# The attention scale moved from the softmax into the weight column of the query latent's norm

## The chip, the core and the metric

The kernel runs on one core of one Trainium2 chip. The metric is the device time of one execution in microseconds; the figure of a kernel is the median of its runs. The engines are named as in the profile: PE is the matrix engine (PEld its weight load), DVE the vector engine, ACT the scalar engine, POOL and SP the two others, of which SP issues most of the DMAs.

## The reference

Two decoder layers on a sequence of 1024 tokens of width 1024, in fp32. Layer 0 is an mLSTM mixer and an MLP; layer 1 is multi-head latent attention and an MLP. The part that matters here is the attention of layer 1: a latent of the query (384 wide) is normalised with a learned weight, projected to 8 heads of 128 plain and 64 rotary columns, and compared with the keys; the scores are scaled, masked and put through a softmax.

```python
cq = rmsnorm(h @ w_q_a, g_q_latent)
q = (cq @ w_q_b).reshape(B_, S, B_HEADS, B_NOPE + B_ROPE)
...
scale = (B_NOPE + B_ROPE) ** -0.5
...
s = (jnp.einsum('bqhd,bkhd->bhqk', qn_b, k_nope)
     + jnp.einsum('bqhd,bkd->bhqk', qr_b, k_rope)).astype(jnp.float32) * scale
s = jnp.where(kpos[None, :] <= qpos[:, None], s, -jnp.inf)
p = jax.nn.softmax(s, axis=-1)
```

## The kernel before

The sequence is worked in two halves of 512 tokens. Nearly every product is done in three passes of a reduced format (a number is split into a high and a low part): `mm3` (L279 to L282) issues high by high, high by low and low by high into the same bank. `wsplit` makes the two parts of a weight, with a cast on ACT (L238) and a subtraction on DVE (L239); `split_mod` does the same for activations (L499 and L500).

From about 990 us on, the attention of one half of the sequence is woven with the MLP of another: `two_streams` (L2771) takes steps of a dense stream (MLP products) and of the other stream (the mixer of layer 1) in turn. Each step's instructions on PE are tied behind the last PE instruction of the step before (`tc.issue_after` in `go`, L2754), so that the order on PE is largely written by hand. What DVE, ACT and the DMA queue on SP do in between is put in order by a planner when the kernel is built (`schedule_with_timeline_sim=True`, L2934): it plays the program through with estimated durations, and gives each engine the ready instruction of the best priority. The priority follows the order of tracing; what is wrapped in `prompt` (L244) or `evac` goes 300 places ahead (`PRIO`). An instruction that is traced late but ready early may so run far ahead of its place.

The query latent `cq` is made in `latent` (L1605): three projections, a reciprocal root mean square (`rstd`), and at L1706 the product with `col(QL + m, 1)` and `rstd`. `col` cuts columns out of the tile `cols`, into which L330 turns the learned vectors at the start; columns 194 to 196 (`QL`) hold `g_q_latent`, one column for 128 of its 384 entries. The split latent then goes through the projections of `kq`, `rot` (first half) or `prepare_pair` (second half) to the plain and the rotary queries, and in `score_mm` (L1770) to the scores: four products of the parts (L1781 to L1784), the mask as a product of an identity with `maskA` (L1786; -1e30 where a key is hidden), and the high by high product (L1787). The scores of one block of 128 queries stay in a bank pair `pm` of PSUM, of which there are two; the MLP uses the same two.

`softmax` (L1789) runs on 128 queries by n keys: a row maximum, negated (L1791, DVE); its product with the scale (L1792, DVE, 128 x 1); the exponential with the scale as immediate factor and the product as bias, which also sums (L1793, ACT); the reciprocal of the sum (L1794) and the product with it (L1795, both DVE). `scores` (L1797) calls it 64 times, under `prompt`: for the first half (`attention_first`, n from 128 to 512, two softmaxes to one `pm`) and for the second (`attention_second`, n from 640 to 1024, one to a `pm`). The result is turned in blocks of 128 by PE (L1901, L1915, L1988) and multiplied with the values.

`rope_perm` (L1521) fills three permutation matrices in `selW` on DVE (L1524 to L1526) from the identity. It is traced once (L2842), after the stretch that works beside the last sweep of the MLP of layer 0 and ahead of both attentions.

Of the kernel before, what the change touches and what calls it, by code (L numbers as in the profile page):

```python
# [13 lines left out]
AF = mybir.ActivationFunctionType  # L14
ALU = mybir.AluOpType
# [67 lines left out]
def kernel(  # L83
# [27 lines left out]
    nc = tc.nc  # L111
# [32 lines left out]
    def small(n, dt=F32):  # L144
        return sb.tile([P, n], dt, tag=f"sm{n}", bufs=6, name=f"sm_{next(uid)}")
# [7 lines left out]
    def pm():  # L153
        return pp.tile([P, 2, 512], F32, tag="pm", bufs=2, name=f"pm_{next(uid)}")
# [177 lines left out]
    col = lambda i, n: cols[:, i : i + n]  # L332
    NG = lambda l, i: col(l * 32 + i * 8, 8)
    AB, KVB, KVG, HG, KVL, QL, GB = 64, 160, 176, 184, 192, 194, 197
# [1184 lines left out]
    both, both_perm = selW[:, 1], selW[:, 2]  # L1519

    def rope_perm():  # L1521
        for q in range(4):
            s = ts(q, 32)
            nc.vector.tensor_copy(perm[:, s], ident[:, ts(q ^ 1, 32)])  # L1524
            nc.vector.tensor_add(both[:, s], ident[:, s], ident[:, ts(q ^ 2, 32)])
            nc.vector.tensor_add(both_perm[:, s], ident[:, ts(q ^ 1, 32)], ident[:, ts(q ^ 3, 32)])  # L1526
# [186 lines left out]
    SCALE = float((128 + 64) ** -0.5)  # L1713
# [75 lines left out]
    def softmax(f, pr, n):  # L1789
        m, l = small(1), small(1)  # L1790
        nc.vector.reduce_max(m, f, axis=AX.X, negate=True)  # L1791
        nc.vector.tensor_scalar(m, m, SCALE, None, ALU.mult)  # L1792
        nc.scalar.activation(pr[:, :n], f, AF.Exp, bias=m, scale=SCALE, accum_out=l)  # L1793
        nc.vector.reciprocal(l, l)  # L1794
        nc.vector.tensor_scalar(pr[:, :n], pr[:, :n], l, None, ALU.mult)  # L1795

    def scores(kk, unit):  # L1797

        (_, q, kn, _), j = unit
        prs = []  # L1800
        if j < 2:
            st = pm()
            pr = raw().rearrange("p (a b) -> p a b", b=512)
            for e in range(2):
                score_mm(lambda g: st[:, e], kk, q, kn, 2 * j + e)
            for e in range(2):
                n = (2 * j + e + 1) * P
                prompt(softmax)(st[:, e, :n], pr[:, e], n)
                prs.append(pr[:, e])
        else:  # L1810
            for e in range(2):
                st = pm()
                n = (2 * j + e + 1) * P
                score_mm(lambda g: st[:, g], kk, q, kn, 2 * j + e)
                pr = raw()
                prompt(softmax)(st.rearrange("p a b -> p (a b)")[:, :n], pr, n)
                prs.append(pr)
        return prs
# [598 lines left out]
    m = [pm(), pm()]  # L2417
# [422 lines left out]
    two_streams(f0, behind(bg_latent(), 5))  # L2840
    apart[0] = False
    rope_perm()  # L2842


# [93 lines left out]
```

## Time and profile before

| what | value |
|---|---|
| time, median of 3 runs | 2321.11 us (2319.03 to 2321.47) |
| the profiled execution | 2317.84 us |
| its span, first to last instruction | 2316.1 us |
| granted clock of PE, mean | 0.997 |
| first and last softmax (start of L1791) | 992.9 and 1771.4 us |
| L1791, 64 times, median | 0.754 us |
| L1793, 64 times, median | 0.744 us |

The profile is of one execution, which was 3.27 us shorter than the median of the others. Times in it count from the span's start. "Idle before, released by" names, for each group, what ended the time in which the engine had nothing to do; a wait for several semaphores is put down to the one that came last.

### The profile page before, as it was taken

How to read it: one execution, taken by the hardware profiler on the slowest of the kernel's cores; microseconds unless marked ns; L12 is line 12 of the kernel's file. 1: busy time of each engine (PE TensorE's matmuls, PEld its weight loads, DVE VectorE, ACT ScalarE, POOL GpSimd, SP SyncE). 2: the span in 40 equal slices, each digit the busy share in tenths (PEclk: the TensorE clock that was granted, in tenths of full speed). 3: DMA queues.
4: the chain of work that ended last, by engine and by line, in shares of the span. 5: the costliest groups of instructions: out<-in, count | busy, mean ns of one | idle time of the engine just before them, and what ended most of it. 6: DMA issues, size and time to landing. Idle time of an engine off the chain costs nothing.

```text
span 2316.1 us, 32512 instructions
## 1 busy us (share of the span) xinstructions
PE 2276.3 (98%) x12010; PEld 1918.0 (83%) x12010; DVE 1698.5 (73%) x2782; ACT 1126.6 (49%) x1919; POOL 84.1 (4%) x164
## 2 busy tenths in 40 slices
PE   8999999999999999999999999999999999999998
PEld 6888788888887878778888788888888888989997
DVE  6676777889887877777765687666666388788776
ACT  4365435765334445545444555433444354555453
POOL 1000000001122210000000000000000000000000
PEclk9999999999999999999999999999999999999999
DMA  9543464668999887656775654764324352445432
GB/s 314 180 129 112 135 182 154 196 221 266 329 282 295 284 293 259 195 187 204 242 253 192 225 197 151 254 230 157 129 95 157 107 168 82 153 144 176 125 110 110
DMA packets 401647, 444.36 MB, mean 192 GB/s; under 512 B 27123, under 2 KB 289328, under 8 KB 401488
## 3 DMA queue, kind: packets, MB, share of 16 engines
q1 hardware_dynamic: 388544, 397.09, 53.6%
q0 software_dynamic: 12944, 45.20, 5.3%
q8 instruction: 94, 1.54, 0.3%
q14 instruction: 65, 0.53, 0.1%
HBM read 343.65 MB, written 98.57 MB: 191 GB/s over the span
## 4 chain that ended last, share of the span: by engine, by line
PE 75%; DMA 9%; DVE 9%; issue 4%; ACT 2%; POOL 0%; SPq 0%; DVEq 0%; ACTq 0%; POOLq 0%
PE ps L280 13%; PE ps L282 13%; PE ps L281 13%; PE pm L280 8%; PE pm L281 8%; PE pm L282 8%; DMA raw<-in_mlp_w_dram 4%; PE pc L281 2%; PE pc L280 2%; PE pc L282 2%; DMA raw<-s 1%; DVE wl L239 1%; DVE k L247 1%; PE pc L1988 1%; DVE sm L1791 1%
## 5 line engine op out<-in xcount | busy, mean ns | idle before, releaser
L238 ACT CAST wh<-raw 128x1024 fp32r<-128x1024 f32 (+2 forms) x317 | 321.4, 1016 | 437.2 <-PE ps L281 177.4
L239 DVE TENSOR_TENSOR wl<-raw,wh 128x1024 fp32r<-128x1024 f32 (+2 forms) x317 | 375.3, 1186 | 202.6 <-ACT wh L238 169.9
L280 PE MATMUL ps<-k,wh 128*128 128x512 f32 (+1 forms) x1252 | 476.0, 380 | 4.8 <-DVE tmc L1084 1.4
L282 PE MATMUL ps<-k,wl 128*128 128x512 f32 (+1 forms) x1252 | 468.4, 374 | 0.5 <-DVE wl L239 0.5
L281 PE MATMUL ps<-k,wh 128*128 128x512 f32 (+1 forms) x1252 | 467.9, 374 | 0.0
L280 PEld LDWEIGHTS ps<-k,wh 128*128 128x128 f32 x1252 | 236.2, 189 | 51.9 <-issue 2.8
L282 PEld LDWEIGHTS ps<-k,wl 128*128 128x128 f32 x1252 | 236.0, 189 | 43.4 <-DVE wl L239 1.0
L281 PEld LDWEIGHTS ps<-k,wh 128*128 128x128 f32 x1252 | 236.3, 189 | 41.4 <-issue 1.4
L247 DVE TENSOR_TENSOR k<-k,pm 128x512 f32<-128x512 f32 (+1 forms) x250 | 192.5, 801 | 63.3 <-PE pm L282 62.8
L280 PE MATMUL pm<-wh,hd 128*128 128x512 f32 x488 | 193.5, 396 | 3.5 <-ACT raw L1793 2.3
L282 PE MATMUL pm<-wh,hd 128*128 128x512 f32 x488 | 190.5, 390 | 0.0
L281 PE MATMUL pm<-wl,hd 128*128 128x512 f32 x488 | 190.3, 390 | 0.0
L280 PEld LDWEIGHTS pm<-wh,hd 128*128 128x128 f32 x488 | 91.7, 188 | 25.3 <-ACT raw L1793 4.6
L282 PEld LDWEIGHTS pm<-wh,hd 128*128 128x128 f32 x488 | 91.6, 188 | 19.9 <-DVE hd L500 0.5
L281 PEld LDWEIGHTS pm<-wl,hd 128*128 128x128 f32 x488 | 91.8, 188 | 18.4 <-issue 0.5
L390 DVE SCALAR_TENSOR_TENSOR tma<-raw,cond,tma 128x512 f32<-128x512 f32 x120 | 89.6, 747 | 16.6 <-DMA raw<-in_ada_w_dram 7.8
L281 PE MATMUL pm<-hd,wk 128*128 128x512 f32 x256 | 100.0, 391 | 1.7 <-DVE hd L500 1.7
L1793 ACT ACTIVATE raw<-pm,sm 128x128 f32<-128x128 f32 (+3 forms) x64 | 47.6, 743 | 111.0 <-DVE sm L1792 106.4
L280 PE MATMUL pm<-hd,wk 128*128 128x512 f32 x256 | 100.9, 394 | 0.6 <-ACT hd L499 0.6
L280 PE MATMUL pm<-hd,wh 128*128 128x512 f32 x256 | 99.2, 389 | 1.1 <-ACT hd L499 1.1
L282 PE MATMUL pm<-hd,wl 128*128 128x512 f32 x256 | 99.8, 390 | 0.1
L281 PE MATMUL pm<-hd,wh 128*128 128x512 f32 x256 | 99.6, 390 | 0.2 <-DVE hd L500 0.2
(497 smaller groups left out, 4828.1 us busy)
## 6 DMA issues: line engine op xcount, KB each, us to landing
raw<-in_mlp_w_dram SPq DMA_DIRECT2D x176, 512.0 KB, 4.5
raw<-in_ada_w_dram SPq DMA_DIRECT2D x64, 512.0 KB, 4.6
raw<-in_mlp_w_dram SPq DMA_DIRECT2D x128, 256.0 KB, 4.7
raw<-in_a_w_in_dram SPq DMA_DIRECT2D x44, 512.0 KB, 4.5
lo<-wl POOLq DMA_DIRECT2D x32, 512.0 KB, 6.1
wk<-lo SPq DMA_DIRECT2D x64, 256.0 KB, 4.4
xs<-k SPq DMA_DIRECT2D x40, 256.0 KB, 4.7
raw<-in_a_w_out_dram SPq DMA_DIRECT2D x16, 512.0 KB, 4.9
```

What stands on the lines that cost most here:

```text
L238: nc.scalar.copy(hi[:, :n], r[:, :n])
L239: i = nc.vector.tensor_sub(lo[:, :n], r[:, :n], hi[:, :n].bitcast(F32))
L247: return f(*a, **k)
L280: nc.tensor.matmul(o, lh, rh, start=start, stop=False)
L281: nc.tensor.matmul(o, lh, rl, start=False, stop=False)
L282: pe_last[0] = nc.tensor.matmul(o, ll, rh, start=False, stop=stop)
L390: nc.vector.scalar_tensor_tensor(acc, r[kk], cond[:, k : k + 1], acc, ALU.mult, ALU.add)
L1791: nc.vector.reduce_max(m, f, axis=AX.X, negate=True)
L1793: nc.scalar.activation(pr[:, :n], f, AF.Exp, bias=m, scale=SCALE, accum_out=l)
L1988: nc.tensor.transpose(pt[:, ts(m, P)], u.prs[i][:, ts(kb, P)], ident)
```

## The change

The scale (192 to the power -0.5) is multiplied once into the three `QL` columns, in `rope_perm`; L1706 then gives a latent, and with it queries and scores, that carry it already. The product at L1792 is dropped, the exponential takes the negated maximum as its bias and no scale.

```diff
     def rope_perm():
+        nc.vector.tensor_scalar(col(QL, 3), col(QL, 3), SCALE, None, ALU.mult)
         for q in range(4):
             s = ts(q, 32)
             nc.vector.tensor_copy(perm[:, s], ident[:, ts(q ^ 1, 32)])
...
     def softmax(f, pr, n):
         m, l = small(1), small(1)
         nc.vector.reduce_max(m, f, axis=AX.X, negate=True)
-        nc.vector.tensor_scalar(m, m, SCALE, None, ALU.mult)
-        nc.scalar.activation(pr[:, :n], f, AF.Exp, bias=m, scale=SCALE, accum_out=l)
+        nc.scalar.activation(pr[:, :n], f, AF.Exp, bias=m, accum_out=l)
         nc.vector.reciprocal(l, l)
         nc.vector.tensor_scalar(pr[:, :n], pr[:, :n], l, None, ALU.mult)
```

## The prediction

> **What bounds the kernel now.** I read the top of the page first, then its chain of waits, then who waited for whom on TensorE (PE).
>
> ```profile
> span 2316.1 us, 32512 instructions
> PE 2276.3 (98%) x12010; PEld 1918.0 (83%) x12010; DVE 1698.5 (73%) x2782; ACT 1126.6 (49%) x1919; POOL 84.1 (4%) x164
> PE 75%; DMA 9%; DVE 9%; issue 4%; ACT 2%; POOL 0%; SPq 0%; DVEq 0%; ACTq 0%; POOLq 0%
> ```
>
> PE is busy for 98% of the span and makes up 75% of the chain that ended last. Only 2316.1 - 2276.3 = 39.8 us are PE idle. A change that takes nothing from PE, as this one, can win at most part of these, and only where the softmax is what PE waits for. The waits of PE on the lines of the softmax (L1791 to L1795), and its longest wait of all:
>
> ```profile
> PE pc L280 <- DVE hd L500: 3.7, 1, 3.7
> PE pm L280 <- ACT raw L1793: 2.3, 4, 1.0
> PE pc L1915 <- DVE raw L1795: 1.4, 1, 1.4
> PE pc L1988 <- DVE raw L1795: 1.3, 6, 0.4
> PE ps L280 <- DVE sm L1792: 1.0, 1, 1.0
> PE pc L1901 <- DVE raw L1795: 0.4, 1, 0.4
> ```
>
> The columns are us in total, times, longest. The five softmax rows make 2.3 + 1.4 + 1.3 + 1.0 + 0.4 = 6.4 us in 13 waits: the whole of what a shorter softmax can win directly. That is 0.28% of the span. All other PE work runs beside the softmax without noticing it, although ScalarE (ACT) does notice:
>
> ```profile
> L1792 DVE TENSOR_SCALAR sm<-sm x64: 141/153/156, 993.2 to 1772.7; 128x1 f32<-128x1 f32 x64
>   ACT raw L1793: 106.4, 50
> ```
>
> The exponential sat 106.4 us behind the product, in 50 of 64 cases. That number is tempting and nearly worthless: ACT is busy for 49% of the span, so most of it is an engine with nothing else to do, waiting for the product only because it came last.
>
> **The change part by part.**
>
> 1. Removed: 64 products on VectorE (DVE), 64 x 0.153 = 9.8 us of durations. DVE is busy for 73% and is not the bound, so this is worth only what it takes off the chain reduce, product, exponential. Without anything between, that step reads:
>
> ```profile
> 992.87 0.28 DVE L1791 TENSOR_REDUCE sm<-pm 128x1 f32<-128x128 f32 x1
> 993.19 0.15 DVE L1792 TENSOR_SCALAR sm<-sm 128x1 f32<-128x1 f32 x1
> 993.46 0.37 ACT L1793 ACTIVATE raw<-pm,sm 128x128 f32<-128x128 f32 x1 [4.35 <-DVE sm L1792]
> ```
>
> The reduce ends at 993.15; the exponential starts at 993.46, 0.31 us later. With the reduce releasing it directly, one handover of 0.12 us (993.34 to 993.46) stays: 0.19 us saved for each softmax.
>
> One rule of the Trainium skill would make this term smaller. "Perfetto Trace Analysis", section Optimizing Scalar/DVE Operations, puts the data-access overhead of a DVE instruction on SBUF at about 60 ns of engine time and says that the profiled latency is about twice this. An estimate from that page with 0.06 in place of 0.19 would bring the sum below to 1.3 us; the rows here show the dependent step at 0.15 + 0.04, so the trace decides against using the smaller figure for a chain.
>
> 2. Moved: in some softmaxes the order of DVE holds other work between reduce and product, which now falls behind the reduce's release.
>
> ```profile
> 1562.19 0.82 DVE L1791 TENSOR_REDUCE sm<-pm 128x1 f32<-128x640 f32 x1
> 1562.92 0.68 DVE L500 TENSOR_TENSOR hd<-tmp,hd 128x512 fp32r<-128x512 f32 x1
> 1563.52 0.14 DVE L1792 TENSOR_SCALAR sm<-sm 128x1 f32<-128x1 f32 x1
> ```
> ```profile
> 1564.70 0.50 PE L280 MATMUL pm<-wh,hd 128*128 128x512 f32 x1 [0.55 <-ACT raw L1793]
> ```
> ```profile
> 999.41 0.56 DVE L1791 TENSOR_REDUCE sm<-pm 128x1 f32<-128x384 f32 x1
> ...
> 1001.61 0.14 DVE L1792 TENSOR_SCALAR sm<-sm 128x1 f32<-128x1 f32 x1
> ```
>
> At 1562 the reduce ends at 1563.01 and the product at 1563.66; the exponential could go 0.65 us earlier, more than the 0.55 us for which PE then waits for the score bank, so that wait goes. At 999 the product came 1.64 us after its reduce, and PE did not wait at all: most of such gaps buy nothing.
>
> 3. Added: one DVE product on 128x3 values in rope_perm, as long as L1792's 0.15 us. It reads the columns that L330 writes, and L1706 is its first reader.
>
> ```profile
> L330 DVE COPY cols<-ps x1: 233/233/233, 15.7 to 15.7; 128x72 f32<-128x72 f32 x1
> L1524 DVE CAST selW<-ident x4: 171/172/174, 268.2 to 268.5; 128x32 fp32r<-128x32 f32 x4
> L1706 DVE SCALAR_TENSOR_TENSOR k<-k,cols,tmc x6: 742/745/752, 959.1 to 1431.4; 128x512 f32<-128x512 f32 x6
> 17.77 0.16 DVE L2334 TENSOR_TENSOR ada<-pc,cols 128x2 f32<-128x2 f32 x1 [1.27 <-PE pc L2330]
> ```
>
> L1524, traced in the same function, runs at 268.2 us, far ahead of where it is traced: the planner fills DVE's gaps with any ready instruction. The new product is ready at 15.9 us and I expect it soon after, in a gap such as the 1.27 us ahead of 17.77. Hidden there it costs 0; without that cover 0.15 us. Its reader is on DVE too, over 900 us later: no new wait on another engine. No DMA is added or moved by the edit, and no queue is crossed; the exponential loses an immediate factor and keeps its bias column, so I take its duration as unchanged.
>
> 4. The sum. Pm waits: 0.55 in full and 0.19 for each of the three others, 1.1. L1988: six of 0.19, 1.1 of 1.3. L1915: its unit holds two softmaxes in one tile, both products ahead of it, 2 x 0.19 = 0.4. L1901 and L280 behind L1792: 0.2 each. Together 3.0 us; the bounds are 0 (PE gives it back at its next wait) and 6.4 (all thirteen waits go). What is late next is PE itself. The profiled execution took 2317.84 us (span 2316.1), the median of the runs is 2321.11, 3.3 us more; I carry the difference over: 2317.84 - 3.0 = 2314.8 in the profile's terms, 2318.1 in those of the median.
>
> 5. The plan. Removing 64 instructions makes the planner place everything from the first softmax on anew on DVE, ACT and the DMA queue, while PE's order is largely tied by hand. The dearest place of the changed stretch is this:
>
> ```profile
> 1010.46 0.62 ACT L499 CAST hd<-tmp 128x512 fp32r<-128x512 f32 x1
> ...
> 1012.62 1.05 ACT L1211 CAST wk<-raw 128x1024 fp32r<-128x1024 f32 x1 [1.54 <-DMA raw<-in_mlp_w_dram]
> ...
> 1013.57 0.96 ACT L499 CAST hd<-pc 128x384 fp32r<-128x384 f32 x2
> ...
> 1014.07 1.18 DVE L500 TENSOR_TENSOR hd<-pc,hd 128x384 fp32r<-128x384 f32 x2 [0.93 <-ACT hd L499]
> ...
> 1014.78 0.77 PE L280 MATMUL pc<-k,wh 128*128 128x512 f32 x1 [3.73 <-DVE hd L500]
> ```
> ```profile
> 1020.81 0.39 PE L282 MATMUL ps<-k,wl 128*128 128x512 f32 x1
> 1021.04 0.40 PE L280 MATMUL ps<-k,wh 128*128 128x512 f32 x1
> 1021.27 0.39 PE L281 MATMUL ps<-k,wh 128*128 128x512 f32 x1
> ```
> ```profile
> 1010.00:1020.00 10.00, 6.27 (x21) 4.95 (x21) 6.86 (x17) 5.12 (x12) 0.00 (x0) 0.69 0.80 256
> ```
>
> A weight cast stands in ACT's queue ahead of two casts of turned scores, and its transfer is 1.54 us late; everything behind it, PE last, waits. The 3.73 us of PE idle are followed by a granted clock of 0.69 in that slice (sixth figure): from 1014.78 to 1020.81 there are 14 matmul starts after the first, 0.43 us apart, where the next are 0.23 apart (1021.04 to 1021.27). That is 14 x 0.20 = 2.8 us more: 6.5 us for this one place.
>
> "TensorE: Matmul & The Clock Gate", section Part 1, of the Trainium skill states that the clock halves after about 3.4 us of idle and comes back after about 3.4 us of work. By that rule only a stall of this length has the second half of the price; this trace agrees, with 3.73 us of idle and 0.69 granted.
>
> **The rivals.**
>
> The stall at 1011 dissolves as well. The planner puts the cast of the scores ahead of the late weight, or DVE's earlier release moves the transfer forward. For it: the place lies behind the first six softmaxes, so its plan is redone. Against it: the product is not in its chain; DVE sat idle for 0.93 us there. Then 3.0 + 6.5 = 9.5 us go: 2311.6.
>
> Slower: the new plan makes such queues elsewhere. An exponential that the planner now thinks ready earlier is put ahead of a weight cast or an eviction in ACT's order, and blocks it when its own scores are late; the cast is late for PE. For it: ACT already stands waiting for 106.4 us in front of the exponential, so its place in the order is where others are held up. Against it: ACT is half idle. One such place as long as that of 1011 costs 6.5, which the 3.0 won do not cover (+3.5, still within 0.2%); it decides from the second on: 2 x 6.5 - 3.0 = +10.0, 2331.1, or one with nothing won, +6.5.
>
> No effect: every shortened wait comes back at PE's next one, 2321.1, give or take 1.5 for shifts of the plan. That the change does not do what it says I exclude: the latent's column enters both parts of the query, all further steps to the score are linear, and the mask stays far below.
>
> **How the numbers follow.** Forecast 0.40, of which 0.13 beyond 0.2% (4.6 us; about what a measurement of this kernel can tell from no change) as its bound of 6.4 lies past it; the stall gone 0.27; slower 0.25; no effect 0.08, of which 0.02 slower. Faster 0.13 + 0.27 = 0.40, same 0.27 + 0.06 = 0.33, slower 0.25 + 0.02 = 0.27. The forecast's own range is 2314.7 to 2321.1 (6.4 to 0 won). The range given reaches from 2308.2 (6.4 + 6.5 won) to the slower rival's 2331.1.
>
> **What would show it.** Right: L1793 waits for L1791; reduce end to exponential start about 0.12 us where ACT is free; the five softmax rows of PE together near 3.4 us; the new product early in the span; PE's busy time unchanged. The first rival shows as no clock below 0.95 between 1000 and 1050. The slower one shows as a PE wait of over 3 us on a cast or an eviction in the stretch from 990 us on, with ACT behind an exponential. I am wrong in kind if the plan ahead of 990 us has changed too, for then waits count that no softmax touches.

## The result and the profile after

The changed kernel takes 2312.2 us (2309.23 to 2314.56, 6 runs) where the kernel before, run beside it, takes 2319.49 us (2318.23 to 2321.47, 6 runs): a ratio of 0.9969, 95% interval 0.9959 to 0.998, 7.3 us less. Run again later it gave 0.9968 (0.9959 to 0.9977). Its profiled execution took 2309.23 us.

The page of the changed kernel, top and chain:

```profile
span 2307.1 us, 32431 instructions
PE 2272.6 (99%) x12010; PEld 1916.3 (83%) x12010; DVE 1690.6 (73%) x2719; ACT 1126.8 (49%) x1919; POOL 84.3 (4%) x164
PE 80%; DMA 7%; DVE 7%; issue 3%; ACT 2%; SPq 0%; POOL 0%; DVEq 0%; ACTq 0%; POOLq 0%
```

PE's share of the chain rises from 75% to 80%; what left the chain is DVE (9% to 7%) and DMA (9% to 7%). In this kernel the line numbers from L1522 to the maximum are one higher: the maximum is L1792, the exponential is L1793 as before. Who made PE wait, among the lines of the softmax, and at the top the wait that had been its longest (3.7 us):

```profile
PE pc L280 <- DVE hd L500: 3.1, 2, 2.8
PE pm L280 <- ACT raw L1793: 1.1, 2, 0.7
PE pc L1915 <- DVE raw L1795: 0.5, 1, 0.5
```

The rows of the softmax fell from 6.4 us in 13 waits to 1.6 us in 3, further than the 3.4 us that the prediction gave as its sign. The step itself, and the new product:

```profile
991.81 0.28 DVE L1792 TENSOR_REDUCE sm<-pm 128x1 f32<-128x128 f32 x1
992.19 0.37 ACT L1793 ACTIVATE raw<-pm,sm 128x128 f32<-128x128 f32 x1 [4.13 <-DVE sm L1792]
```
```profile
L1522 DVE TENSOR_SCALAR cols<-cols x1: 157/157/157, 16.2 to 16.2; 128x3 f32<-128x3 f32 x1
```
```profile
  DVE sm L1792: 105.1, 47
```

From the end of the reduce (992.09) to the exponential there are 0.10 us, where there were 0.31. The new product runs at 16.2 us, half a microsecond after its columns are written. And ACT's idle time in front of the exponential is 105.1 us, where it was 106.4: the number that looked largest hardly moved. PE's busy time fell by 3.7 us, although the change takes no work from it. An estimate from the granted clock gives as much: 0.83 to 1.00 between 20 and 30 us is 1.7 us, and 0.93 to 0.97 between 990 and 1040 us is 2.0 us.

**Where the time went by stage.** The matmuls of the two profiles come in nearly the same order, so that the same matmul can be looked up in both; the difference of its starts is what has been won up to there. Four such matmuls, first of the kernel before, then of the changed one:

```profile
46.22 0.50 PE L280 MATMUL pm<-k,wh 128*128 128x512 f32 x1 [0.63 <-ACT k L502]
...
959.27 0.50 PE L280 MATMUL ps<-k,wh 128*128 128x512 f32 x1 [1.38 <-DVE tmc L1084]
...
1328.83 0.50 PE L281 MATMUL pm<-hd,wk 128*128 128x512 f32 x1 [1.34 <-DVE hd L500]
...
1956.38 0.50 PE L280 MATMUL pm<-wh,hd 128*128 128x512 f32 x1 [0.15 <-DVE k L247]
```
```profile
44.79 0.51 PE L280 MATMUL pm<-k,wh 128*128 128x512 f32 x1 [0.64 <-ACT k L502]
...
957.73 0.50 PE L280 MATMUL ps<-k,wh 128*128 128x512 f32 x1 [1.38 <-DVE tmc L1084]
...
1324.84 0.50 PE L281 MATMUL pm<-hd,wk 128*128 128x512 f32 x1 [1.33 <-DVE hd L500]
...
1948.29 0.50 PE L280 MATMUL pm<-wh,hd 128*128 128x512 f32 x1 [0.16 <-DVE k L247]
```

Up to the first row 1.43 us are won, up to the second 1.54, to the third 3.99, to the fourth 8.09, and 9.0 over the span. So 1.4 us come from the first 46 us, nothing to speak of from there to 959 us, 2.5 us from the first attention, 4.1 us from the stretch with the second, 0.9 us from the end. The 1.4 us at the start are the granted clock (sixth figure). First the kernel before in that slice, then the changed one, then the changed one in a later profile:

```profile
20.00:30.00 10.00, 9.78 (x61) 6.01 (x54) 5.94 (x11) 4.37 (x8) 0.00 (x0) 0.83 1.07 373
```
```profile
20.00:30.00 10.00, 9.62 (x63) 6.40 (x60) 7.16 (x14) 5.38 (x9) 0.00 (x0) 1.00 1.07 372
```
```profile
20.00:30.00 10.00, 9.84 (x62) 6.11 (x55) 5.96 (x12) 4.38 (x8) 0.00 (x0) 0.83 1.07 373
```

The changed kernel shows 1.00 once and 0.83 once: this is chance from one execution to the next, not the change. Without it the two profiles are 7.6 us of span apart, which fits the 7.3 us of the medians.

A single pair of profiles has more chance in it than that. The changed kernel's later profile has the four matmuls at 46.15, 961.71, 1329.94 and 1952.27 us: 1.3 us won in the first attention and 5.2 in the second, while the stretch from 46 to 959 us, whose instructions are the same, is 2.5 us longer than before. That stretch holds no softmax, and the order on every engine is the same in both kernels up to 995 us (time of the kernel before; there DVE's order is the first to differ), so the sign by which the prediction would have been wrong in kind, a plan changed ahead of 990 us, did not show.

### The profile page after: what moved, and what is told of

Its sections match the earlier page's. It is cut to its first block, busy times and chain, and to the rows that moved or that the text cites. A ratio compares the mean times of both kernels' runs of the same rounds, so it can differ in the third digit from the quotient of the medians.

```text
span 2307.1 us, 32431 instructions
## 1 busy us (share of the span) xinstructions
PE 2272.6 (99%) x12010; PEld 1916.3 (83%) x12010; DVE 1690.6 (73%) x2719; ACT 1126.8 (49%) x1919; POOL 84.3 (4%) x164
## 3 DMA queue, kind: packets, MB, share of 16 engines
q8 instruction: 94, 1.54, 0.3%
## 4 chain that ended last, share of the span: by engine, by line
PE 80%; DMA 7%; DVE 7%; issue 3%; ACT 2%; SPq 0%; POOL 0%; DVEq 0%; ACTq 0%; POOLq 0%
PE ps L280 13%; PE ps L281 13%; PE ps L282 13%; PE pm L280 8%; PE pm L281 8%; PE pm L282 8%; DMA raw<-in_mlp_w_dram 3%; PE pc L282 2%; PE pc L281 2%; PE pc L280 2%; DVE wl L239 1%; DVE k L247 1%; PE pc L1988 1%; DMA tmc<-in_ada_w_dram 1%; PE pm L1788 1%
## 5 line engine op out<-in xcount | busy, mean ns | idle before, releaser
L239 DVE TENSOR_TENSOR wl<-raw,wh 128x1024 fp32r<-128x1024 f32 (+2 forms) x317 | 375.3, 1185 | 201.6 <-ACT wh L238 176.8
L282 PE MATMUL ps<-k,wl 128*128 128x512 f32 (+1 forms) x1252 | 468.3, 374 | 0.5 <-DVE wl L239 0.5
L281 PE MATMUL ps<-k,wh 128*128 128x512 f32 (+1 forms) x1252 | 467.8, 374 | 0.0
L282 PEld LDWEIGHTS ps<-k,wl 128*128 128x128 f32 x1252 | 235.9, 188 | 43.3 <-DVE wl L239 1.0
L281 PEld LDWEIGHTS ps<-k,wh 128*128 128x128 f32 x1252 | 236.2, 189 | 41.4 <-issue 1.4
L282 PE MATMUL pm<-wh,hd 128*128 128x512 f32 x488 | 190.4, 390 | 0.0
L281 PE MATMUL pm<-wl,hd 128*128 128x512 f32 x488 | 190.4, 390 | 0.0
L282 PEld LDWEIGHTS pm<-wh,hd 128*128 128x128 f32 x488 | 91.6, 188 | 19.8 <-DVE hd L500 0.5
L281 PEld LDWEIGHTS pm<-wl,hd 128*128 128x128 f32 x488 | 91.7, 188 | 18.4 <-issue 0.5
L281 PE MATMUL pm<-hd,wk 128*128 128x512 f32 x256 | 100.0, 391 | 1.7 <-DVE hd L500 1.7
L280 PE MATMUL pm<-hd,wk 128*128 128x512 f32 x256 | 100.9, 394 | 0.6 <-ACT hd L499 0.6
L282 PE MATMUL pm<-hd,wl 128*128 128x512 f32 x256 | 99.8, 390 | 0.2 <-DVE wl L239 0.2
L282 PE MATMUL pm<-hd,wk 128*128 128x512 f32 x256 | 99.7, 390 | 0.0
L281 PE MATMUL pm<-hd,wh 128*128 128x512 f32 x256 | 99.6, 390 | 0.2 <-DVE hd L500 0.2
L1793 ACT ACTIVATE raw<-pm,sm 128x128 f32<-128x128 f32 (+3 forms) x64 | 47.7, 745 | 105.4 <-DVE sm L1792 105.1
```

Source lines behind the costliest of these rows:

```text
L239: i = nc.vector.tensor_sub(lo[:, :n], r[:, :n], hi[:, :n].bitcast(F32))
L280: nc.tensor.matmul(o, lh, rh, start=start, stop=False)
L281: nc.tensor.matmul(o, lh, rl, start=False, stop=False)
L282: pe_last[0] = nc.tensor.matmul(o, ll, rh, start=False, stop=stop)
L1793: nc.scalar.activation(pr[:, :n], f, AF.Exp, bias=m, accum_out=l)
```

## The experiments

Three theories stood against each other. A: the product cost time as a link of the chain reduce, product, exponential. B: it cost nothing, and the planner's new order happened to be better. C: it cost the time that it took on DVE. All ratios are to the kernel before, run on the same chip; the changed kernel stands at 0.997.

**The link back, everywhere.**

```diff
         nc.vector.reduce_max(m, f, axis=AX.X, negate=True)
+        nc.vector.tensor_scalar(m, m, 1.0, None, ALU.mult)
         nc.scalar.activation(pr[:, :n], f, AF.Exp, bias=m, accum_out=l)
```

> The scale stays in the weight column, and the product comes back between reduce and exponential with a factor of 1.0, in all 64 softmaxes. Theory A (the link in the chain reduce, product, exponential is what PE paid for): the gain is gone, 0.9985 to 1.0015 of the kernel before, and PE's waits on the softmax lines are back at 5 to 7 us. Theory B (the planner's new order is what won, the link costs nothing by itself): the time can be anywhere between 0.995 and 1.003, and need not go back. Theory C (64 instructions less on DVE are what won): also 1.000.

Measured: 2319.76 us against 2320.06, ratio 1.000 (0.9991 to 1.0008). PE's waits on the softmax lines are back at 7.5 us in 13. The gain is gone although the scale stays in the weight column: the arithmetic of the change is worth nothing by itself, the missing instruction is. It fits A and C, and of B only a version in which the order hangs on this instruction.

**The link back in one attention.** The same line under `if n <= 512:` (first attention), then under `if n > 512:` (second).

> The product with 1.0 comes back only where n is at most 512, the 32 softmaxes of the first attention. From the two traces, matched matmul by matmul, the second attention won 4.3 us and the first 2.2. Theory A: the second's part stays, 4.3 of 2319.5 us, about 0.998; PE's waits for L1988 between 1550 and 1800 us stay under 0.3 us. Theory B: no tie between place and gain. Theory C: half of the gain, 0.9985.

> The product with 1.0 comes back only where n is above 512, the 32 softmaxes of the second attention. Theory A: PE's six waits for L1988 (1.3 us together) and the waits on the score bank (2.3 us) are back between 1550 and 1800 us, and only the first attention's 2.2 us stay, about 0.999. Theory B: no tie. Theory C: half of the gain, 0.9985.

Measured: 0.9989 (0.998 to 0.9998) with the link in the first attention, 0.9983 (0.9975 to 0.9992) with it in the second. As differences to the kernel before, 2.5 us are won where only the second attention is free of it, and 3.9 us where only the first is; together 6.4 of the 7.3 us, with an interval of some 2 us to either side of each. Each attention has its part; which of the two is larger these intervals do not tell. The profiles tell more: the starts of the same matmuls give the length of the stretch with the first attention (second to third row above) and of the one with the second (third to fourth row). All profiles of this document whose matmuls run at the same pace, in us:

| links in that attention's softmaxes | stretch of the first attention | stretch of the second |
|---|---|---|
| none | 367.0 to 369.2 (6 profiles), mean 367.8 | 622.3 to 623.5 (6), mean 623.0 |
| one | 369.6 to 375.1 (4), mean 372.6 | 625.5 to 627.6 (4), mean 626.7 |
| two (a run below) | 378.5 (1) | 628.8 (1) |

The ranges do not overlap in either column. By the means one link costs about 4.9 us in the first attention and 3.7 us in the second, together 8.6 us, inside the interval of the result. The pair of the result had shown 2.5 us for the first because the profile of the kernel before is the shortest of its row. The waits are tied to the link as well. The waits of the weight load (PEld) on the softmax lines, in the stretch of each attention: first with the link in the first attention only, 985 to 1270 us and 1500 to 1800 us, then with the link in the second only, the same two stretches:

```profile
PEld pc L1917 <- DVE raw L1797: 2.8, 2, 1.7
PEld ps L280 <- DVE sm L1794: 1.1, 1, 1.1
PEld pc L1903 <- DVE raw L1797: 0.6, 1, 0.6
```
```profile
PEld pm L280 <- ACT raw L1795: 1.6, 3, 1.1
PEld pc L1990 <- DVE raw L1797: 0.6, 3, 0.2
```
```profile
PEld pc L1917 <- DVE raw L1797: 0.6, 1, 0.6
```
```profile
PEld pm L280 <- ACT raw L1795: 4.0, 7, 1.4
PEld pc L1990 <- DVE raw L1797: 2.9, 7, 0.5
```

(Lines are two higher here.) 4.5 and 2.2 us with the link in the first, 0.6 and 6.9 with it in the second, where the kernel before has 3.6 and 7.5 and the changed one 1.0 and 3.1: where the link is, the waits are.

**The products beside the chain.** All 64 products run on DVE, into a column that nobody reads; the exponential takes the reduce's result.

```diff
+    junk = const([P, 1], F32, "junk")
...
+        nc.vector.tensor_scalar(junk, m, 1.0, None, ALU.mult)
         nc.scalar.activation(pr[:, :n], f, AF.Exp, bias=m, accum_out=l)
```

> All 64 products run again on DVE, but into a column that nobody reads, so that the exponential waits for the reduce alone: DVE's time is as before the change, the chain as after it. Theory A: nearly the whole gain stays, 0.997 to 0.998. Theory C: the gain is gone, 1.000. Theory B: anywhere between 0.995 and 1.003.

Measured: 1.0046 (1.0032 to 1.006), slower than any theory gave. The waits did not explain it: all of PE's waits together were 24.1 us, less than in the changed kernel (26.5). Looked up matmul by matmul, 8 of the 18 us by which its profile is longer were there at 960 us, before the first softmax: the matmuls themselves were slower, those of 512 columns 230.8 ns from start to start on average where the kernels before and after have 227.5 (distances of over 320 ns left out). The new tile moves every tile set up behind it by its size. So the run said nothing on A and C, and two others had to part them: the products into a spare column of a tile that is there anyway (`cols[:, 247:248]` in place of `junk`), and the tile without the products (one memset, never read).

> The 64 products beside the chain once more, now into column 247 of a tile that is there anyway and has 48 columns to spare, so that no tile changes its address. Theory A (the link in the chain is the price): nearly the whole gain stays, 0.996 to 0.998, matmuls of 512 columns 227.5 ns apart as in the kernels before and after. Theory C (DVE's time is the price): 1.000.

> The changed kernel with one more tile of one column, written once and not read; it shifts the addresses of tiles that are set up after it. If the 230.8 ns between matmuls of the run with products into a tile of its own came from the shifted addresses, they are here too, and the time is 12 to 20 us above the changed kernel, 1.002 to 1.006. If they came from the products, matmuls are 227.5 ns apart and the ratio is 0.997.

Measured: the products in place 0.9964 (0.9952 to 0.9977), matmuls 227.5 ns apart; the tile alone 1.0027 (1.0015 to 1.0038), matmuls 230.8 ns apart. C falls: with 64 products back on DVE the whole gain is there, as long as they are not between reduce and exponential. (In this run PE's longest wait, 3.8 us, is put down to the product in the spare column; it stands where the changed kernel waits 2.8 us for the split at L500, and is no wait for the softmax.) And most of the loss of the run before came with the tile and not with the products: the tile alone shows the slower matmuls; whether the products add to it, the intervals of the two runs leave open. One of the groups that carry it, in the changed kernel and in the one with the tile (us in total, mean ns):

```profile
L281 PE MATMUL ps<-k,wh 128*128 128x512 f32 x1060 | 413.4, 390 | 0.0
```
```profile
L281 PE MATMUL ps<-k,wh 128*128 128x512 f32 x1060 | 419.6, 396 | 0.0
```

**Two links.** Two products with 1.0 one after the other.

> Two products with 1.0, one after the other, between reduce and exponential in all 64 softmaxes. Theory A: the second link costs about as much as the first did, 4 to 8 us more than the kernel before, 1.002 to 1.0035, with PE's softmax waits at 9 us and more. Theory B: no order between one and two links.

Measured: 1.0033 (1.002 to 1.0045), by the medians 7.0 us above the kernel before, about as much again as the first link costs. PE's waits on the softmax lines: 12.0 us in 15. Zero, one and two links give 0.997, 1.000 and 1.0033. This dose, in order and in size, leaves no room for B as pure luck of the order.

**The added part alone.** The kernel before with a product by 1.0 on the three columns in `rope_perm`.

> The kernel before with the added part alone: one product with 1.0 on the three columns, the softmax as it was. By both theories 0.9995 to 1.0005 if the product falls into a gap near 16 us, as in the changed kernel; more than 0.2% either way would mean that one instruction is enough to turn the plan.

Measured: 0.9996 (0.9987 to 1.0005). The added instruction costs nothing that can be measured, and it does not turn the plan: on every engine all other instructions stand in the order of the kernel before.

**Two attempts at the rest of the stall.** The splits of the turned probabilities were put 300 places ahead, in the first attention, then in both; the changed kernel ran beside them. One of the calls (the others are changed in the same way):

```diff
-                        split_mod(PTh[s], PTl[s], pv, None)
+                        prompt(split_mod)(PTh[s], PTl[s], pv, None)
```

> The changed kernel, and in the first attention the splits of the turned probabilities go 300 places ahead too. What is left of the stall at 1012.8 us (2.8 us of idle, half of it with a lower clock behind it) is PE waiting for these splits, which stand behind the MLP's squares in ACT's order. If that order is the cause: the stall falls under 1 us and the granted clock stays at 1.00 there, 2 to 4 us below the changed kernel, about 0.995 of the one before. If it is the transfer's landing, nothing changes, 0.997. The other side: the squares come late for PE instead, 0.998 to 1.001.

> The same in both attentions. In the second, PE does not wait for the splits of turned probabilities in the changed kernel, so the second attention should give nothing beyond the run with the first alone: equal to it within 0.1%; a loss of 0.2% or more would show that casts of weights are pushed back by it.

> The changed kernel itself beside the two, for a direct comparison: 0.996 to 0.998 of the kernel before. Half clock between 20 and 25 us was seen in two of six profiles; if it is chance and not the change, it need not be absent here.

Measured: 0.9968 (0.9957 to 0.998), 0.9969 (0.9957 to 0.9981), and 0.9968 (0.9959 to 0.9977) for the changed kernel: no difference. The expectation of less than 1 us of stall missed. The order on ACT that it was to break is the same as it was:

```profile
1010.66 1.05 ACT L1211 CAST wk<-raw 128x1024 fp32r<-128x1024 f32 x1 [1.09 <-DMA raw<-in_mlp_w_dram]
1011.62 0.61 ACT L499 CAST hd<-u 128x512 fp32r<-128x512 f32 x1
1012.14 0.63 ACT L980 ACTIVATE tmp<-tmp 128x512 f32<-128x512 f32 x1
1012.80 0.63 ACT L981 ACTIVATE tmp<-tmp 128x512 f32<-128x512 f32 x1
1013.33 0.35 ACT L1936 COPY tmp<-ps 128x256 f32<-128x256 f32 x1
1013.59 0.62 ACT L499 CAST hd<-tmp 128x512 fp32r<-128x512 f32 x1
1014.10 0.97 ACT L499 CAST hd<-pc 128x384 fp32r<-128x384 f32 x2
```

The two casts that PE waits for (the last row) still come behind the MLP's, so whether that order is the cause of the rest was not tested and stays open. No version tried beats the changed kernel.

## Why the prediction was right or wrong

The direction was right, and the range held the time. The size was not: 3.0 us were forecast for the direct effect, 7.3 were measured. The interval (4.6 to 9.5 us) leaves out the 3.0; the forecast's own bound of 6.4 lies inside it, below the middle. The number of the first rival (9.5 us, the direct effect and the stall gone) is nearer than the forecast's, its mechanism only half true. That the range held the time owes something to its width, which came from the rivals.

**The link's 0.19 us** (step 1): 0.21 in the same place (0.31 to 0.10). Right; so was going by the trace and not by the 0.06 us.

**The sum** (step 4) is the step that failed: it took 0.19 us off most waits, 3.0 in all, from rows that did not hold the whole price. Three things came out larger. First, PE's own rows fell by 4.8 us and not by 3.0: 2.5 in the second attention, where 2.2 were counted, and 2.3 in the first (2.8 to 0.5), where 0.8 were counted. Why single waits of the first attention shrank by more than their links was not looked into. Second, the meter: I took the whole of what a shorter softmax can win from the rows of PE, 6.4 us. The rows of the weight load in the same view give more, for the kernel before and the changed one:

```profile
PEld pm L280 <- ACT raw L1793: 4.6, 7, 1.4
PEld pc L1988 <- DVE raw L1795: 2.9, 7, 0.6
PEld pc L1915 <- DVE raw L1795: 1.7, 1, 1.7
...
PEld ps L280 <- DVE sm L1792: 1.4, 1, 1.4
...
PEld pc L1901 <- DVE raw L1795: 0.5, 1, 0.5
```
```profile
PEld pm L280 <- ACT raw L1793: 2.5, 5, 1.1
...
PEld pc L1915 <- DVE raw L1795: 1.0, 2, 0.7
...
PEld pc L1988 <- DVE raw L1795: 0.6, 3, 0.2
```

11.1 us before, 4.1 after: 7.0 us, against 6.4 and 1.6 by PE's rows, 4.8 us. In these rows a wait for the softmax is 0.1 to 0.4 us longer on the weight load than on the matmul (1.7 and 1.4 at L1915), and three of the seven weight loads that wait for the exponential have no waiting matmul beside them. For the second attention alone PEld's rows went from 7.5 to 3.1 us, 4.4, close to the 4.1 of the matched matmuls; PE's rows gave 3.6 to 1.1, 2.5. Two links take PEld's rows there from 7.5 to 8.7 us, and the stretch is 1.3 us longer. "Perfetto Trace Analysis", section Identifying the Most-Contended Engine, of the Trainium skill says that matmul busy time is a poor measure because matmuls are pipelined, and asks for the busy share of the weight load, beside the share of peak arithmetic. It says nothing of waits; that the same holds for them, the rows of the second attention show (4.4 against 2.5).

For the whole kernel the 7.0 us come near the 7.3 in part by luck: in the first attention the rows of neither engine hold what the clock takes. There two links raise PEld's rows by 2.0 us, and the stretch is 9 us longer. This is the third part, a term that I had put at nothing: the granted clock behind the first attention's own waits. The wait at L1915 and the clock around it, in the run with the added product alone (softmax as before), then in the profile of the kernel before:

```profile
998.90 0.44 PE L1916 MATMUL pc<-ident,raw 128*128 128x128 f32 x2 [1.50 <-DVE raw L1796]
990.00:1010.00 20.00, 18.28 (x85) 14.46 (x84) 15.26 (x34) 8.39 (x17) 0.00 (x0) 0.91 0.43 133
```
```profile
996.67 0.44 PE L1915 MATMUL pc<-ident,raw 128*128 128x128 f32 x2 [1.36 <-DVE raw L1795]
990.00:1010.00 20.00, 18.64 (x104) 15.46 (x102) 16.47 (x37) 10.34 (x21) 0.00 (x0) 1.00 0.50 165
```

The three other profiles with a link in the first attention show 0.91 in this stretch too, behind a wait of 1.5 to 3.0 us; the kernel before, the one that I read, and all eight without the link show 1.00. A clock of 0.91 over 20 us is an estimated 1.8 us, which no row of waits has.

**The wait at 1564** (step 2) was to go; 0.40 of its 0.55 us stayed. The exponential did start 0.03 us after its reduce, in place of 0.75. But that reduce stood on DVE behind a weight's subtraction (L239, 1.23 us) which follows a transfer and not PE; so it came only 3.63 us earlier (1562.19 to 1558.56), while PE came 4.20 earlier. I had held the rest of the chain fixed to PE.

**The added product** (step 3): right, at 16.2 us and free, also alone.

**The plan** (step 5 and the first rival). I argued against the rival that the product is not in the chain of the stall at 1011 us. That holds for its data, but not for the queue. The load that the late cast waited for, first before, then after:

```profile
1001.85 0.95 SPq L260 DMA_DIRECT2D raw<-in_b_w_q_b_dram  x2
...
1005.86 1.38 SPq L1209 DMA_DIRECT2D raw<-in_mlp_w_dram  x2
```
```profile
995.68 0.91 SPq L260 DMA_DIRECT2D raw<-in_b_w_q_b_dram  x2
...
1001.82 0.99 SPq L1209 DMA_DIRECT2D raw<-in_mlp_w_dram  x2
```

The new order lets it go 4.0 us earlier; its cast starts at 1007.63 in place of 1012.62, after a wait of 1.14 us for the transfer, and from there to the late casts ACT works without a break. The stall is 2.81 us in place of 3.73, and fewer matmuls behind it run at half pace. It did not go: the clock between 1010 and 1020 us is 0.83, below the 0.95 that the prediction gave as the rival's sign. The stretch is tied to the link in the first attention, and not only in these two profiles. The stretch from 990 to 1040 us, with the link in both attentions, in the first only, in the second only, and in none (the changed kernel):

```profile
990.00:1040.00 50.00, 42.58 (x207) 34.83 (x206) 35.29 (x73) 21.11 (x41) 0.00 (x0) 0.90 0.50 160
```
```profile
990.00:1040.00 50.00, 43.27 (x211) 35.41 (x210) 37.28 (x77) 21.38 (x43) 0.00 (x0) 0.93 0.51 163
```
```profile
990.00:1040.00 50.00, 46.55 (x233) 38.24 (x232) 38.36 (x75) 23.60 (x48) 0.00 (x0) 0.97 0.61 188
```
```profile
990.00:1040.00 50.00, 45.87 (x231) 37.53 (x230) 37.71 (x75) 23.87 (x49) 0.00 (x0) 0.97 0.61 188
```

With the link in the first attention, five profiles have this stall at 3.6 to 5.3 us and a granted clock of 0.90 to 0.93 in the stretch; without it, eight have 2.2 to 4.2 us and 0.97 to 1.00. So the clock parts the two groups, and the length of the stall alone does not: 3.6 us is the run with two links, 3.8 us the run with the products in place, 4.2 us the run with `junk`, whose matmuls are slower throughout. Nor is the length a matter of the plan alone, since the kernel before and the run with the added product have the same order everywhere and stalls of 3.7 and 5.3 us. The 0.97 to 1.00 against 0.90 to 0.93 includes the clock behind the wait at L1915. PE's rows (2.3 us) and an estimate from the clock (0.04 to 0.07 of 50 us, 2 to 3.5 us) together come near the 4 to 5 us of the first attention, where I had counted 0.8. How much of it is the earlier load and how much the shorter chain ahead of it no run parts.

**The slower rival** did not show: no wait of PE of over 3 us came up anywhere from 990 us on.

## What to carry to other kernels

In this kernel a tiny instruction costs what its place costs: 64 products of 0.15 us were worth 7.3 us between reduce and exponential, and nothing beside the chain, on the same engine. Read the waits of a busy matrix engine on the weight load too, and not on the matmul alone; in the second attention its rows had the gain within 0.3 us (4.4 against 4.1), and matmul rows missed a third of it. Then look at the granted clock behind the waits: in the first attention no row of waits held the price. And do not take a gain by stage from one pair of profiles, since the stretch from 46 to 959 us, with the same instructions, took between 912.3 and 916.3 us in the eleven profiles whose matmuls run at the same pace. An engine's large idle time (106.4 us of ACT) said nothing here of what a shorter wait was worth. And where an experiment needs a buffer, take it out of one that is there.

## What the runs showed of the hardware

One added tile of 128 x 1 made matmuls of 512 columns 1.5% slower on average (227.5 to 230.8 ns apart), some 14 us of the run (1.0027 against 0.9968 of the kernel before), with nothing but one memset besides. Only some groups feel it (`ps<-k,wh` at L281 390 to 396 ns, `pm<-wh,hd` at L282 390 and 391). That points to where their operands lie, which is not shown, and which property of the address would decide was not tried.

The granted clock fell behind shorter idle stretches than the 3.73 us of the prediction: behind 1.50 us in the run with the added product alone, behind 2.17 us with the link in the second attention only, behind 2.81 us in the changed kernel; and it stayed at 1.00 behind 1.36 us in the kernel before and behind 2.77 us where the splits were put ahead in the first attention. The rule of the Trainium skill quoted in the prediction ("TensorE: Matmul & The Clock Gate", Part 1: about 3.4 us of idle) is therefore no bound below which a stall is safe here.
